# A planned single-core kernel gets new instruction costs, a clock for its DMAs, and other places for the first loads

## The chip, the cores and the metric

The kernel runs on one core of a Trainium2 chip. The metric is the device time of one execution in microseconds (us); smaller is better. TensorE (PE) multiplies, VectorE (DVE), ScalarE (ACT) and GpSimd (POOL) do the elementwise work, and SyncE (SP) issues every DMA.

## The reference

Two transformer-like blocks run one after the other on 512 tokens of width 2048, in float32. The first block: a memory of 256 rows is normalised and projected to keys and values; the tokens are normalised and projected to a gated delta-rule branch, to cross-attention queries and to a gate z; the gated result goes through an output projection and is added to the tokens. The second block does the same with an mLSTM and an HGRN2 branch, then adds `sigmoid(rmsnorm(h) @ w_pg) * (p @ w_pe)` and ends in a root-mean-square norm.

```python
mem_n = rms_norm(mem, mem_norm_g)
h = rms_norm(x, norm_g[i])
proj = jnp.einsum("bsd,de->bse", h, dn_w_in[j])
...
kv = jnp.einsum("bmd,de->bme", mem_n, w_kv)
...
y = jnp.concatenate([mix, xa], axis=-1) * jax.nn.silu(z)
x = x + jnp.einsum("bse,ed->bsd", y, w_out[i])
...
gate = jax.nn.sigmoid(jnp.einsum('bsd,de->bse', rmsnorm(h, pe_norm_w[l]), w_pg[l]))
h = h + gate * e
out = rmsnorm(h, final_norm_w)
```

## The kernel before, in words

Activations lie with features on the partitions and the 512 tokens along the free axis. A weight matrix is a list of jobs of 128 output columns each. A job's weights come in pieces of four 128x128 blocks (256 KB); ACT rounds a piece to `hi`, DVE takes the rest `lo`, and each block gives three matmuls (hi by the activation's high part, hi by its low part, lo by its high part) into one PSUM bank. Six raw pieces (`RAW`) may be on their way and five split pieces (`SPL`) may be ready.

No engine decides the order at run time. While the program is built, `Driver.run` plays a greedy planner: it keeps one clock for each engine (`clk`), adds a written cost for every instruction (`_on`), and emits the next instruction whose inputs are ready by these clocks, matmul units of the projections when nothing of higher priority is ready. Each engine then executes its own list strictly in this order, so an instruction that waits on the chip holds up all behind it on its engine. `calm` holds back optional work while ACT or DVE runs ahead of PE by the planner's clocks. All DMAs go out on SP's one queue, also in this order.

The opening. `first_loads` puts the eight loads of the memory (`mraw`, 256 KB each) after the first weight pieces and the sixteen loads of the tokens (`xraw`, 256 KB each) after the next sixteen. `mem_task` rounds the memory and sums its squares; `x_task` squares each token tile on ACT, adds it to `xsum` on DVE, and hands the normalised parts (`part`) to the query projection. The jobs of `w_k` come first, the first two of them interleaved piece by piece; then `w_v`, then `w_xq`. Until `w_xq` starts, PE multiplies with 256 columns of memory alone.

The middle. Twelve groups of the delta rule each need the inverse of eight 32x32 triangular blocks at once: `inverse` runs 31 steps on DVE, each a multiply and a `tensor_reduce` that needs it, then two transposes whose result `Dt` PE multiplies into tile `pp`. The planner gives a step's instructions these costs, and frees the engine for others after every third step.

The end. The jobs of `w_pg` fill the gate. For the last three tiles they are cut into two halves of 256 tokens, so that the final norm of the first half overlaps the matmuls of the second. `out_half` scales sixteen tiles: on POOL as a tensor_tensor for those of `on_pool`, whose weight ACT multiplied in before (`evac_g`), on DVE as a scalar_tensor_tensor for the rest.

Of the kernel before, what the change touches and what calls it, by code (L numbers as in the profile page):

```python
# [38 lines left out]
def v4(ap):  # L39
    return ap.rearrange("p (n c) -> p n c", n=NCH)  # L40

# [37 lines left out]
class Driver:  # L79
# [5 lines left out]
    def __init__(self, tc, wp, psp, sp):  # L85
        self.tc, self.nc, self.wp, self.psp, self.sp = tc, tc.nc, wp, psp, sp
        self.clk = dict(pe=0.0, act=0.0, dve=0.0, pool=0.0)
# [12 lines left out]
        self.nslot = 0  # L100
        self.table = None
        self.nhead, self.head = 0, None
# [8 lines left out]
    def act(self, out, in_, func, table=None, **kw):  # L111
        t = table or {AF.Exp: 1, AF.Ln: 1, AF.Silu: 2, AF.Sigmoid: 3}.get(func)
        cost = 0.11 + free_size(out) / 1200
        if t and t != self.table:
            self.table = t
            cost += 1.3
# [6 lines left out]
    def _v(self, eng, n):  # L123
        if eng is None:
            self._on("dve", 0.08 + n / 960, LV)
            return self.nc.vector
        self._on("pool", 0.1 + n / 400, LV)
        return eng

    def tt(self, out, a, b, op, eng=None):  # L130
        self._v(eng, free_size(out)).tensor_tensor(out=out, in0=a, in1=b, op=op)  # L131

    def stt(self, out, a, s, b, op0, op1):
        self._v(None, free_size(out)).scalar_tensor_tensor(out=out, in0=a, scalar=s, in1=b, op0=op0, op1=op1)  # L134

    def ts(self, out, a, s1, op0, s2=None, op1=None, eng=None):
        kw = dict(op1=op1) if op1 is not None else {}
        self._v(eng, free_size(out)).tensor_scalar(out=out, in0=a, scalar1=s1, scalar2=s2, op0=op0, **kw)

    def cp(self, out, a, eng=None):  # L140
        self._v(eng, free_size(out)).tensor_copy(out=out, in_=a)

    def set(self, out, v, eng=None):
        self._v(eng, free_size(out)).memset(out, v)

    def keep(self, out, in_, sign, fill):
# [5 lines left out]
        self._on("pool", 0.2 + n * c / 1200, LV)  # L152

    def scan(self, out, a, b, init, op0, op1):
        self._v(None, free_size(out)).tensor_tensor_scan(out=out, data0=a, data1=b, initial=init, op0=op0, op1=op1)

    def mm(self, out, lhsT, rhs, start=True, stop=True, tr=False):
        n = free_size(out)
        if lhsT.dtype == F32R:
            c = max(0.107, n / 2400)  # L160
        elif tr:
            c = 0.105
        else:
            c = max(0.055 if lhsT.shape[0] <= 32 else 0.107 if lhsT.shape[0] <= 64 else 0.2, n / 600)
            if lhsT.shape[0] <= 64:
                c = min(c, 0.107)
# [4 lines left out]
    def dma(self, out, in_, lat=2.3):  # L171
        self.nc.sync.dma_start(out=out, in_=in_)
        self.tau = max(self.tau, self.clk["pe"]) + lat
# [92 lines left out]
    def _pump(self):  # L266
        while self.i_dma < len(self.pieces):
# [6 lines left out]
            self.pieces[self.i_dma] = (j, c0, n, raw, max(self.clk["pe"] + 3.0, 4.5 + 1.5 * self.i_dma))  # L274
# [121 lines left out]
def build(ctx: ExitStack, tc: tile.TileContext, A, out):  # L396
# [49 lines left out]

    def first_loads(i):

        if i < len(mraw):
            nc.sync.dma_start(out=mraw[i], in_=A["memT"][:, 2 * i:2 * i + 2])  # L450
        elif i < len(mraw) + KT:
            k = i - len(mraw)
# [4 lines left out]
            d.give(f_x[k])  # L457
            f_x[k].tau = d.clk["pe"] + 3.0

    f_x = [Fut() for _ in range(KT)]  # L460
# [99 lines left out]
    def mem_task():  # L560
        hs = []
        for i, t in enumerate(mraw):
            d.tau = 3.8 + 1.5 * i
# [14 lines left out]
        for i, t in enumerate(mraw):  # L578
            d.tau = t0
            yield from d.calm(AHEAD)  # L580
# [10 lines left out]
    def x_task():  # L591
        ssum = yield from slot(name="xsum")
        for k, t in enumerate(xraw):
            yield from need(f_x[k])
            yield from d.calm(AHEAD)
# [6 lines left out]
            free(q)  # L602
        f = Fut()
# [135 lines left out]
    def evac_ab(job):  # L739
# [22 lines left out]
        d.dma(dgc, rows[0:32])  # L762
# [89 lines left out]
    def inverse(g, Mn):  # L852
# [273 lines left out]
    def y_loader():  # L1126
        yield from need(f_zb0)
        for i in range(KI):
# [8 lines left out]
            yield  # L1137
            d.dma(t, yscr[i])
            give((f_yl if i < 2 * XH else f_yf)[i], t)
        give(f_all)  # L1140
# [122 lines left out]
    def evac_if(job):  # L1263
# [35 lines left out]
        for j, r in enumerate((mu, wi, en)):  # L1299
            d.dma(drow[j], r[0:32], lat=0)  # L1300
        d.dma(dws, ws[:, 0:NCH])
# [8 lines left out]
        d.dma(wsb, bc(dws, 0, 128))  # L1310
# [29 lines left out]
    def ml_task(h):  # L1340
# [4 lines left out]
        for j in range(3):  # L1345
            t = yield from slot(name="rowb")
            yield
            d.dma(t, mlg["drow"][j, h:h + 1].broadcast_to((128, T)))
# [163 lines left out]
    def hg_task(h):  # L1512
# [39 lines left out]
        for l in range(len(LEVELS)):  # L1552
# [19 lines left out]
            elif LEVELS[l] == 1:  # L1572
# [3 lines left out]
                d._on("dve", 0.4, LV)  # L1576
# [114 lines left out]
    def on_pool(k):  # L1691
        return k % 3 == 1 and k < KT - NSP

    def evac_g(i):
        def gen(job):
# [37 lines left out]
    def out_half(c, n, t, last):  # L1733
# [3 lines left out]
        for k0 in range(0, KT, 2):  # L1737
            o = yield from slot((128, 2, n), name="out")
            te = []
            for k in (k0, k0 + 1):  # L1740
# [4 lines left out]
                if on_pool(k):  # L1745
                    tt(o[:, k - k0], h, t, MUL, eng=pool)
# [10 lines left out]
    d.nhead = len(mraw) + KT  # L1757
# [4 lines left out]
    d.add(jk[0], jk[1])  # L1762
    for j in jk[2:] + jv[:-2]:
# [246 lines left out]
```

## Time and profile before

| | us |
|---|---|
| median of 3 runs | 2913.86 |
| lowest and highest | 2908.96 and 2915.22 |
| the profiled execution, its own time | 2909.13 |
| its span from first to last instruction | 2907.3 |

The mean granted clock of TensorE over the span was 0.996 of full speed. A row of a view names the line of the helper that issues an instruction (L167 is every matmul, L120 every ACT instruction, L131 every tensor_tensor), so instructions are told apart by tiles. A square bracket at the end of a timeline row is the engine's idle time before the instruction, and what ended it.

### The profile page before, as it was taken

To read this page: it belongs to the slowest core of one execution; us is meant where nothing else is said; L and a number is where in the kernel's file an instruction comes from. 1 tells how busy PE (TensorE), PEld (TensorE's weight loads), DVE (VectorE), ACT (ScalarE), POOL (GpSimd) and SP (SyncE) were. 2 spreads that over 40 slices of the span, in tenths; PEclk is the share of its full clock that TensorE was granted. 3 is DMA by queue.
4 is the path that set the end of the run, shared out by engine and by line. 5 is a ranking of instruction groups with operands and counts; after the bars stand their busy time and mean duration, and the time that the engine had idled before them with its cause. 6 is when DMAs were issued, how large, how long until landed. Compare 5 with 4: busy or idle time off the path is not lost. (4 is left out here: it accounts for less than half of the span.)

```text
span 2907.3 us, 41141 instructions
## 1 busy us (share of the span) xinstructions
PE 2856.6 (98%) x15032; PEld 2390.5 (82%) x15032; DVE 1722.0 (59%) x3305; ACT 1395.3 (48%) x2636; POOL 81.0 (3%) x180
## 2 busy tenths in 40 slices
PE   8999999999999999999999999999999999999997
PEld 7877887788788888888888878888888888888887
DVE  6746677778777777635333364455655655544446
ACT  6544545555445555435222334445555556433434
POOL 0000100100000100000000000000000000000000
PEclk9999999999999999999999999999999999999999
DMA  7422422233222222354433433222222222333324
GB/s 244 142 80 93 123 93 90 95 101 96 82 93 99 95 98 92 100 168 129 129 118 120 148 110 109 87 81 80 84 80 80 89 86 87 115 119 112 96 94 145
DMA packets 179021, 311.05 MB, mean 107 GB/s; under 512 B 25345, under 2 KB 32129, under 8 KB 178817
## 3 DMA queue, kind: packets, MB, share of 16 engines
q1 hardware_dynamic: 178816, 308.41, 33.4%
q8 instruction: 118, 1.93, 0.3%
q14 instruction: 87, 0.70, 0.1%
HBM read 292.34 MB, written 15.99 MB: 106 GB/s over the span
## 5 line engine op out<-in xcount | busy, mean ns | idle before, releaser
L131 DVE TENSOR_TENSOR lo<-raw,hi 128x512 fp32r<-128x512 f32 (+1 forms) x956 | 643.9, 685 | 618.5 <-ACT hi L120 599.5
L120 ACT ACTIVATE hi<-raw 128x512 fp32r<-128x512 f32 (+1 forms) x964 | 591.6, 621 | 865.0 <-PE acc L167 761.8
L167 PE MATMUL acc<-xh,hi 128*128 128x512 f32 x1424 | 582.4, 409 | 0.7 <-ACT xh L120 0.4
L167 PE MATMUL acc<-xl,hi 128*128 128x512 f32 x1424 | 556.2, 391 | 2.8 <-DVE xl L131 2.7
L167 PE MATMUL acc<-xh,lo 128*128 128x512 f32 x1408 | 551.5, 392 | 4.5 <-DVE lo L131 4.4
L167 PE MATMUL acc<-x2h,hi 128*128 128x512 f32 x1040 | 415.8, 400 | 0.0
L167 PE MATMUL acc<-x2l,hi 128*128 128x512 f32 x1040 | 405.2, 390 | 0.0
L167 PE MATMUL acc<-x2h,lo 128*128 128x512 f32 x1024 | 399.8, 390 | 0.0
L167 PEld LDWEIGHTS acc<-xh,lo 128*128 128x128 f32 x1408 | 264.4, 188 | 63.7 <-DVE lo L131 6.2
L167 PEld LDWEIGHTS acc<-xl,hi 128*128 128x128 f32 x1424 | 268.5, 189 | 54.6 <-DVE xl L131 3.9
L167 PEld LDWEIGHTS acc<-xh,hi 128*128 128x128 f32 x1424 | 268.2, 188 | 53.6 <-issue 1.7
L167 PE MATMUL acc<-ph,hi 128*128 128x512 f32 x768 | 298.8, 389 | 0.0
L167 PE MATMUL acc<-pl,hi 128*128 128x512 f32 x768 | 298.8, 389 | 0.0
L167 PE MATMUL acc<-ph,lo 128*128 128x512 f32 x768 | 298.8, 389 | 0.0
L167 PEld LDWEIGHTS acc<-x2h,lo 128*128 128x128 f32 x1024 | 192.2, 188 | 41.4
L167 PEld LDWEIGHTS acc<-x2h,hi 128*128 128x128 f32 x1040 | 195.6, 188 | 37.2
L167 PEld LDWEIGHTS acc<-x2l,hi 128*128 128x128 f32 x1040 | 195.7, 188 | 36.9
L167 PEld LDWEIGHTS acc<-pl,hi 128*128 128x128 f32 x768 | 144.2, 188 | 30.0
L167 PEld LDWEIGHTS acc<-ph,hi 128*128 128x128 f32 x768 | 144.2, 188 | 29.9
L167 PEld LDWEIGHTS acc<-ph,lo 128*128 128x128 f32 x768 | 144.2, 188 | 29.8
L134 DVE SCALAR_TENSOR_TENSOR cv<-acc,c_dn_conv,cv 128x511 f32<-128x511 f32 x144 | 107.4, 747 | 35.6 <-ACT cv L120 32.1
L131 DVE TENSOR_TENSOR Xb<-Xb,Nb 128x16 f32<-128x16 f32 (+30 forms) x372 | 115.4, 310 | 8.8
(322 smaller groups left out, 3679.8 us busy)
## 6 DMA issues: line engine op xcount, KB each, us to landing
raw<-w_qkv SPq DMA_DIRECT2D x192, 256.0 KB, 3.2
raw<-w_out SPq DMA_DIRECT2D x192, 256.0 KB, 2.9
raw<-w_z SPq DMA_DIRECT2D x128, 256.0 KB, 3.2
raw<-w_pg SPq DMA_DIRECT2D x76, 256.0 KB, 3.1
gR<-dgc SPq DMA_DIRECT2D x48, 256.0 KB, 4.1
raw<-w_k SPq DMA_DIRECT2D x32, 256.0 KB, 4.7
raw<-w_v SPq DMA_DIRECT2D x32, 256.0 KB, 3.6
raw<-w_xq SPq DMA_DIRECT2D x32, 256.0 KB, 3.1
```

The lines of the kernel that those rows point to most:

```text
L120: self.nc.scalar.activation(out=out, in_=in_, func=func, **kw)
L131: self._v(eng, free_size(out)).tensor_tensor(out=out, in0=a, in1=b, op=op)
L134: self._v(None, free_size(out)).scalar_tensor_tensor(out=out, in0=a, scalar=s, in1=b, op0=op0, op1=op1)
L167: self.nc.tensor.matmul(out, lhsT=lhsT, rhs=rhs, start=start, stop=stop, is_transpose=True if tr else None)
```

## The change

The planner's costs are written anew: ACT from PSUM is cheaper and with a per-partition scale dearer; DVE's scalar_tensor_tensor and scan are dearer, its copies and tensor_scalar from SBUF cheaper, its reduce in the inverse cheaper; POOL is split by instruction; a 512-column projection matmul costs 544/2400 us in place of 512/2400, and a switch between small and large matmuls costs 0.15 us. A clock for SP and one for the DMA engines (`land`) say when a load is there; before, a load was taken to be there 2.3 or 3.0 us after PE's clock. The loads of memory and tokens are placed in a list (`loads`) that starts the tokens after the fifth weight piece, between the memory's loads. The first four jobs of `w_k` are interleaved in place of two. The token squares are added on POOL. `y_loader` no longer waits in the planner for one load before it issues the next. At the end, ACT multiplies the final weight into all thirteen whole tiles, so that DVE scales them with tensor_tensor, and one more tile (the thirteenth) goes to POOL.

```diff
-        cost = 0.11 + free_size(out) / 1200
+        cost = (0.055 if in_psum(in_) else 0.105) + free_size(out) / 1200
+        if not all(isinstance(kw.get(k, 0.0), (int, float)) for k in ("scale", "bias")):
+            cost += 0.075
...
     def tt(self, out, a, b, op, eng=None):
-        self._v(eng, free_size(out)).tensor_tensor(out=out, in0=a, in1=b, op=op)
+        n = free_size(out)
+        self._v(eng, 0.07 + n / 960, 0.43 + n / 590).tensor_tensor(out=out, in0=a, in1=b, op=op)
...
         if lhsT.dtype == F32R:
-            c = max(0.107, n / 2400)
+            c = max(0.107, (n + 32) / 2400)
...
+        if small != self.small_mm:
+            self.small_mm = small
+            c += 0.15
...
+    def land(self, n=128 * T, extra=0.1):
+
+        t = max(self.clk["pe"], self.clk["sp"])
+        self.clk["sp"] = t + 0.5
+        self.dq = max(self.dq, t + 2.0)
+        self.dq += (0.7 if self.dq > 9 else 1.1) * n / (128 * T)
+        return self.dq + 0.25 + extra
...
+    loads = [[] for _ in range(1 + 3 * KT)]
+    for i in range(len(mraw)):
+        loads[4 * (i // 2) + (i % 2 if i < 2 else i % 2 - 1)].append(("m", i))
+    n = 0
+    for i in range(len(loads)):
+        if n < KT and (i % 4 in (1, 2) and i > 4 if i < KT else i >= KT):
+            loads[i].append(("x", n))
+            n += 1
...
             if k == 0:
-                cp(ssum, q)
+                cp(ssum, q, eng=pool)
             else:
-                tt(ssum, ssum, q, ADD)
+                tt(ssum, ssum, q, ADD, eng=pool)
...
-        d._on("dve", 1.2, LV)
+        d._on("dve", 2.0, LV)
...
             nc.vector.tensor_reduce(out=Xb[:, :, i], in_=pr[:, :, 0:i + 1], op=ADD, axis=AX.X)
-            d._on("dve", 0.33 + 8 * (i + 1) / 960, LV)
+            d._on("dve", 0.07 + 8 * (i + 1) / 960, LV)
...
     def on_pool(k):
-        return k % 3 == 1 and k < KT - NSP
+        return k % 3 == 1 and k < KT - NSP or k == KT - NSP - 1
...
-                if on_pool(i):
-                    act(h, h, AF.Copy, scale=w[:, i:i + 1])
+                act(h, h, AF.Copy, scale=w[:, i:i + 1])
...
-                if on_pool(k):
-                    tt(o[:, k - k0], h, t, MUL, eng=pool)
+                if k < KT - NSP:
+                    tt(o[:, k - k0], h, t, MUL, eng=pool if on_pool(k) else None)
...
-    d.add(jk[0], jk[1])
-    for j in jk[2:] + jv[:-2]:
+    d.add(*jk[:4])
+    for j in jk[4:] + jv[:-2]:
```

## Rows read from the trace of the kernel before

**Rows 1.** The page: the span, and busy time of each engine.
```profile
span 2907.3 us, 41141 instructions
...
PE 2856.6 (98%) x15032; PEld 2390.5 (82%) x15032; DVE 1722.0 (59%) x3305; ACT 1395.3 (48%) x2636; POOL 81.0 (3%) x180
```

**Rows 2.** PE's waits, 0 to 131 us: total, times, longest.
```profile
PE acc L167 <- ACT mh L120: 7.1, 1, 7.1
PE acc L167 <- DVE lo L131: 3.9, 2, 2.7
PE acc L167 <- ACT hi L120: 2.5, 1, 2.5
PE acc L167 <- DVE xl L131: 1.9, 1, 1.9
```

**Rows 3.** Windows of the opening: each engine's busy time (instructions), clock, DMA.
```profile
10.00:20.00 10.00, 7.54 (x53) 7.34 (x51) 5.77 (x12) 5.81 (x13) 0.00 (x0) 0.95 0.92 309
20.00:30.00 10.00, 10.00 (x62) 9.78 (x62) 9.79 (x18) 9.88 (x20) 0.00 (x0) 0.71 0.95 332
30.00:40.00 10.00, 8.79 (x74) 8.58 (x73) 7.03 (x13) 6.29 (x12) 0.00 (x0) 1.00 0.80 259
40.00:50.00 10.00, 7.25 (x58) 6.84 (x57) 6.21 (x15) 7.32 (x17) 0.00 (x0) 0.99 0.64 218
50.00:60.00 10.00, 10.00 (x73) 10.00 (x74) 8.36 (x16) 4.70 (x9) 0.00 (x0) 0.84 0.65 213
60.00:70.00 10.00, 10.00 (x86) 10.00 (x85) 7.20 (x15) 6.66 (x13) 0.00 (x0) 1.00 0.51 155
```

**Rows 4.** Timeline around the first token tile: SP's issue, then ACT.
```profile
15.22 0.33 SPq L456 DMA_DIRECT2D xraw<-xT  x1
...
18.33 0.63 ACT L120 ACTIVATE xsq<-xraw 128x512 f32<-128x512 f32 x1 [3.51 <-DMA xraw<-xT]
```

**Rows 5.** Windows of the middle: columns as above (PE, PEld, DVE, ACT, POOL).
```profile
325.00:1207.00 882.00, 869.70 (x5259) 720.98 (x5258) 685.13 (x1558) 476.25 (x1031) 63.23 (x143) 1.00 0.29 94
...
1700.00:2500.00 800.00, 794.81 (x3960) 667.39 (x3959) 456.09 (x775) 407.35 (x687) 4.71 (x12) 1.00 0.28 87
```

**Rows 6.** PE's waits, 131 to 2880 us: one row of eleven.
```profile
PE acc L167 <- DVE xl L131: 0.8, 1, 0.8
```

**Rows 7.** Timeline of DVE, an inverse: start, duration, instruction.
```profile
561.47 0.25 DVE L131 TENSOR_TENSOR Xb<-Xb,Nb 128x88 f32<-128x88 f32 x1
561.76 0.25 DVE L881 TENSOR_REDUCE Xb<-Xb 128x8 f32<-128x88 f32 x1
562.04 0.26 DVE L131 TENSOR_TENSOR Xb<-Xb,Nb 128x96 f32<-128x96 f32 x1
```

**Rows 8.** Timeline of DVE and PE where that inverse ends.
```profile
591.37 0.45 DVE L900 STREAM_TRANSPOSE Dt<-Dt 128x256 f32<-128x256 f32 x1
...
591.91 0.57 PE L167 MATMUL pp<-Dt,gR 32*32 32x32 f32 x25 [0.48 <-issue]
```

**Rows 9.** PE's waits, 2880 us to the end.
```profile
PE ss L167 <- DVE gt L131: 2.6, 1, 2.6
PE acc L167 <- DVE lo L131: 2.0, 1, 2.0
```

**Rows 10.** Timeline of POOL and DVE: the final scaling, and a lone tensor_tensor pair.
```profile
2881.73 2.83 POOL L131 TENSOR_TENSOR out<-h1r,gt 128x256 f32<-128x256 f32 x4 [390.25 <-ACT gt L120]
2896.40 3.31 POOL L131 TENSOR_TENSOR out<-h1r,gt 128x256 f32<-128x256 f32 x4 [11.84 <-ACT gt L120]
...
2888.49 4.04 DVE L134 SCALAR_TENSOR_TENSOR out<-h1r,c_fin_w,gt 128x256 f32<-128x256 f32 x10
...
2896.35 6.80 DVE L134 SCALAR_TENSOR_TENSOR out<-h1r,c_fin_w,gt 128x256 f32<-128x256 f32 x12 [0.86 <-ACT gt L120]
...
40.10 0.75 DVE L131 TENSOR_TENSOR xk<-acc,mraw 128x256 f32<-128x256 f32 x2
```

More of the change, by code (lines that the diff above doesn't have):

```diff
@@ L40, in v4, with in_psum @@
     return ap.rearrange("p (n c) -> p n c", n=NCH)
+def in_psum(ap):
+    return ap.tensor.space == "PSUM"
 def free_size(ap):
@@ L101, in __init__ @@
         self.table = None
+        self.small_mm = False
         self.nhead, self.head = 0, None
@@ L151, in keep @@
             compare_op=ALU.is_ge if sign > 0 else ALU.is_gt, fill=fill)
-        self._on("pool", 0.2 + n * c / 1200, LV)
+        self._on("pool", 0.1 + n * c / 1050, LV)
     def scan(self, out, a, b, init, op0, op1):
-        self._v(None, free_size(out)).tensor_tensor_scan(out=out, data0=a, data1=b, initial=init, op0=op0, op1=op1)
+        self._v(None, 0.07 + free_size(out) / 460, 0).tensor_tensor_scan(
+            out=out, data0=a, data1=b, initial=init, op0=op0, op1=op1)
     def mm(self, out, lhsT, rhs, start=True, stop=True, tr=False):
         n = free_size(out)
+        small = max(lhsT.shape[0], free_size(lhsT)) <= 64
         if lhsT.dtype == F32R:
-            c = max(0.107, n / 2400)
+            c = max(0.107, (n + 32) / 2400)
         elif tr:
-            c = 0.105
-        else:
-            c = max(0.055 if lhsT.shape[0] <= 32 else 0.107 if lhsT.shape[0] <= 64 else 0.2, n / 600)
-            if lhsT.shape[0] <= 64:
-                c = min(c, 0.107)
+            c = 0.109
+        elif small:
+            c = 0.035 if lhsT.shape[0] <= 32 else 0.11
+        else:
+            c = max(0.222, (n + 5) / 600)
+        if small != self.small_mm:
+            self.small_mm = small
+            c += 0.15
         self.nc.tensor.matmul(out, lhsT=lhsT, rhs=rhs, start=start, stop=stop,
@@ L169, in mm, with dma @@
         self._on("pe", c, LP)
-    def dma(self, out, in_, lat=2.3):
+    def land(self, n=128 * T, extra=0.1):
[4 more added lines that the diff above has]
+        return self.dq + 0.25 + extra
+    def dma(self, out, in_, extra=0.9, n=128 * T):
         self.nc.sync.dma_start(out=out, in_=in_)
-        self.tau = max(self.tau, self.clk["pe"]) + lat
+        self.tau = max(self.tau, self.land(n, extra))
     def slot(self, shape=(128, T), dt=F32, name="s", reserve=0):
@@ L273, in _pump @@
             self.nc.sync.dma_start(out=raw[:, :n, :j.w.shape[2]], in_=j.w[:, c0:c0 + n])
-            self.pieces[self.i_dma] = (j, c0, n, raw, max(self.clk["pe"] + 3.0, 4.5 + 1.5 * self.i_dma))
+            self.pieces[self.i_dma] = (j, c0, n, raw, self.land(n * 128 * j.w.shape[2]))
             self.i_dma += 1
@@ L445, in build @@
         xraw.append(d.slot_now(name="xraw"))
-    def first_loads(i):
[L449 to L452, printed above, removed]
+    loads = [[] for _ in range(1 + 3 * KT)]
[6 more added lines that the diff above has]
+            n += 1
+    def first_loads(i):
+        for what, k in loads[i] if i < len(loads) else ():
+            if what == "m":
+                nc.sync.dma_start(out=mraw[k], in_=A["memT"][:, 2 * k:2 * k + 2])
+                f_m[k].tau = d.land()
+                f_m[k].done = True
+                continue
             if k == 0:
@@ L456, in first_loads @@
             nc.sync.dma_start(out=xraw[k], in_=A["xT"][:, k])
-            d.give(f_x[k])
-            f_x[k].tau = d.clk["pe"] + 3.0
+            f_x[k].tau = d.land(extra=0.5)
+            f_x[k].done = True
+    f_m = [Fut() for _ in mraw]
     f_x = [Fut() for _ in range(KT)]
@@ L562, in mem_task @@
         for i, t in enumerate(mraw):
-            d.tau = 3.8 + 1.5 * i
+            d.tau = 0.0
+            yield from need(f_m[i])
             yield
@@ L579, in mem_task @@
             d.tau = t0
+            yield from need(f_m[i])
             yield from d.calm(AHEAD)
@@ L592, in x_task @@
         ssum = yield from slot(name="xsum")
+        tp = 0.0
         for k, t in enumerate(xraw):
+            d.tau = 0.0
             yield from need(f_x[k])
+            yield
             yield from d.calm(AHEAD)
@@ L761, in evac_ab @@
         yield
-        d.dma(dgc, rows[0:32])
+        d.dma(dgc, rows[0:32], n=32 * T)
         pt = yield from transpose4(rows)
@@ L1756, in build @@
     d.head = first_loads
-    d.nhead = len(mraw) + KT
+    d.nhead = len(loads) - 1
     d.spawn(mem_task(), 1)
```

38 lines of the change are left out of this document (24 added, 14 removed).

## The prediction, made before the changed kernel ran

> **What bounds the kernel now.** I read the page first: PE is busy for 2856.6 us of a span of 2907.3 us [rows 1]. The change leaves the matmuls as they are, in number and shape, so it can only win what PE stands idle or runs slowly, some 50 us in all, and it can lose without such a limit. The next view is therefore PE's waits, by stretch, with the windows beside them. They fall into four places.
>
> The first 7.1 us are the wait for the first loads [rows 2]; they stay, since the first load of memory and the first weights go out as before.
>
> The opening behind it: with the memory's 256 columns a window of 10 us holds 86 matmuls when nothing is short (60 to 70 us), 0.116 us each. The five windows before it hold 53, 62, 74, 58 and 73 [rows 3]; 130 are missing, 15 us at that price, less the matmuls that PE was still too cold to make early in the first window. The window at 20 us has no idle time at all and still holds only 62: the granted clock there is 0.71, so part of the stretch ran at the lower of the two levels (1.2 in place of 2.4 GHz), right behind PE's wait of 2.5 us. A wait here is paid nearly twice.
>
> The middle, 325 to 2500 us: PE is idle for 882.0 - 869.7 = 12.3 us and 800.0 - 794.8 = 5.2 us [rows 5], single waits of at most a few us, 17.5 us together.
>
> The end: two waits of 2.6 and 2.0 us [rows 9], and then the final scaling, 6.8 us on DVE after PE's last result [rows 10].
>
> **Part 1, where the first loads stand.** The wait of 2.5 us is for `hi`, and the reason stands on ACT: the square of the first token tile was put in front of it, the tile's load was issued at 15.22 us, and ACT stood 3.51 us until 18.33 us for it [rows 4]. The planner had taken the load to be there 3.0 us after PE's own clock, which runs ahead of a loaded DMA queue. With `land` the square is emitted by a clock that counts the loads in front of it, and the first tokens go out after the fifth weight piece. I take this wait as gone with the slow clock behind it: 2.5 us and 24 missing matmuls x 0.116 = 2.8 us, together 5.3 us.
>
> From 30 to 60 us 12 + 28 + 13 = 53 matmuls are missing, 6.2 us. These are two waits for `lo` [rows 2], 3.9 us, and the slow clock behind the second (0.84). They come from the evacuation of the key jobs, whose norm DVE waits for with `lo` queued behind it. The change leaves `evac_k` alone and, with four jobs that end together, puts two such norms close to each other; against that, four jobs use each memory tile for twice the work before PE needs the next. Bounds 0 and 6.2; I credit 2.7, a little under half.
>
> Four interleaved jobs ask less of the DMA, not nothing. Up to the sixteenth weight piece 16 + 8 + 6 = 30 loads of 256 KB go out. At 332 GB/s and a DMA share of 0.95, what the busiest window shows, one takes 0.79 us and thirty 23.7 us, while PE has 192 matmuls x 0.116 = 22.3 us of work. So DMA stays just the slower; I charge 1.5 us.
>
> The tokens must be ready for `w_xq`. Now PE waits 1.9 and 0.8 us for `xl` [rows 2, 6]. In the plan DVE is freed of sixteen adds, and PE's written cost is 6% higher (544 against 512), so optional work passes `calm` earlier. But PE will also come there earlier. Bounds 0 and 2.7; I credit 1.8.
>
> **Part 2, the token sums on POOL.** The end of the kernel shows what two engines do to each other. POOL alone takes 2.83 / 4 = 0.71 us for a 256-column tensor_tensor, beside DVE 3.31 / 4 = 0.83. DVE alone takes 4.04 / 10 = 0.40 us for its scaling; of the last twelve, eight at 0.40 leave 3.6 us for the four that meet POOL, 0.90 each [rows 10]. So one POOL instruction of 256 columns costs DVE 0.5 us, one of 512 an estimated 1.0, and sixteen 16 us; the adds that leave DVE were worth 16 x 0.75 = 12 us (0.75 us is the pair of 256 columns in rows 10). DVE ends up with 4 us more, not less, inside a stretch where it was busy 9.79 of 10 us once [rows 3]. The five split pieces in reserve are worth 5 x 12 x 0.116 = 7 us of PE, so I charge nothing beyond the 1.5 us; without that reserve it is the rival B.
>
> The Trainium skill (SBUF — State Buffer, Who interferes with whom) says that a DVE instruction with two SBUF inputs and a GpSimd instruction that reads SBUF exclude each other, the second blocked until the first is finished. By that rule DVE's instruction would take 0.40 + 0.71 = 1.11 us where the trace has 0.90, and the sixteen sums would cost DVE 23 us in place of 16; the direction agrees, the size is smaller here.
>
> **Part 3, the written costs.** They move no work, only the order. For most instructions the direction is plain from the diff. One goes astray. In the inverse a multiply and the reduce behind it took 562.04 - 561.47 = 0.57 us for 88 elements [rows 7], each waiting for the one before. The old costs say 0.08 + 0.33 + 2 x 88/960 = 0.59, the new ones 0.14 + 0.18 = 0.32. Over 31 steps the planner will hold DVE free 7.7 us too early. What takes this up: after each third step it waits 0.3 us for the result, then for the end of a unit of three matmuls (0.68 us, on average half of it), some 0.6 us x 10 = 6 us, if no other work fills these gaps; DVE is busy for 685 of 882 us there. So at the end of an inverse DVE is late by about 2 us, at most 7.7. There is no reserve behind it: `Dt` ended at 591.82 and PE began `pp` at 591.91 [rows 8], having waited for it. What is late there stops PE. Against 2 us stand the coarser steps of everything else; I charge 0.7 us for each of twelve inverses, 8 us, with bounds 0 and 12 x 4 = 48. The 17.5 us of idle time in the middle come from the old plan's errors, and a new order removes some and makes others: credit 6, bounds 0 and 17.5. The middle: +2 us.
>
> **Part 4, the end.** DVE's ten scalings of the first half stand in front of the `gt` that PE's last sum waits for; as tensor_tensor they cost 0.375 in place of 0.40 us, and one fewer is left, about 0.4 us. After the last sum POOL has five tiles, 5 x 0.83 = 4.15 us, in which DVE makes 4.6 of its eleven; the other 6.4 (three of them at 0.40) take 2.5 us: 6.65 against 6.80. The wait of 2.0 us for `lo` depends on where that piece falls in DVE's list; I credit 0.5 (bounds 0 and 2.0). Together -1.1 us. The nine added products on ACT, 9 x 0.63 = 6 us, lie beside `w_pg` matmuls, with ACT busy for 48% of the span; without that cover they cost these 6 us. The burst of `y` loads that the planner now allows takes SP's queue, but weights are fetched six pieces ahead; nothing.
>
> **The sum.** Opening -5.3 - 2.7 - 1.8 + 1.5 = -8.3; middle +2; end -1.1: -7.4 us. The profiled execution took 2909.1 us, so 2901.7 by its scale; the median of the runs shown is 4.7 us above it, and against the median I say 2906.5.
>
> **The rivals.** A, slower: the short-costed inverse. If DVE is late by 3 us at each, PE loses 36 us, and with the other terms (-8.3, -6, -1.1) the kernel takes 2913.9 + 20.6 = 2934.5. It decides from 15.4 / 12 = 1.3 us an inverse upwards. For it: rows 7 and 8. Against it: PE's waits of now for `pp` are 0.5 us, and the gaps of rows 5. B, no change: POOL's sums hold `lo` back in the opening, where DVE has no room, and PE's waits come back in another place with their slow clock; the opening gives 2 us: 2912.8. For it: 9.79 us busy; against: the windows from 30 us on, with DVE at 6 to 8. C, more: nearly all waits of the middle vanish as well: -8.3 - 15 - 1.1 = 2889.5. For it: these waits are faults of the plan; against: an instruction planned to be just in time has no reserve. D, the clock doesn't do what it says: `land` counts 0.7 us a load where the window shows 0.79, so after 46 loads it is 4 us early and ACT again stands before a token tile; the opening gives 3 us: 2911.8.
>
> **How the numbers follow.** Forecast 0.46 (its own range 2900 to 2912.5), A 0.24, B 0.10, C 0.14, D 0.06. About 0.2% (6 us) is what a measurement of this kernel can tell from no change. Faster by more: C and four fifths of the forecast, 0.51; within it: B, D and the rest of the forecast, 0.25; slower: A, 0.24. The range 2888 to 2932 leaves out the far part of A and a little of C.
>
> **What would show it.** Right: no ACT idle time on a token load before 25 us; 75 or more matmuls in the windows from 20 us on, clock near 1; the first `w_xq` matmul some 8 us earlier; POOL busy about 20 us more; DVE instructions of 0.9 us beside it. Wrong: new waits of PE for `pp`, `up` or `pst` on DVE between 325 and 1207 us, more than 12.3 us of idle time there (A); waits for `lo` before 60 us as long as now (B, D).

## The result and the profile after

The changed kernel is slower: a median of 2939.65 us (2939.21 to 2941.61) against 2914.54 us for the kernel before, a ratio of 1.0093 with a 95% interval of 1.0078 to 1.0108. The forecast was 2906.5 in a range of 2888 to 2932; the time lies outside it, on the other side of the kernel before. Rival A (2934.5) came nearest. The marks below are read from one profiled execution of each kernel. Executions of one and the same kernel differ by up to 8 us, so a difference of a few us between two marks says little by itself.

The profiled execution has a span of 2938.1 us, 30.8 more than before (the medians differ by 25.1; the profiled execution of before was one of its shorter ones). The page after, span and busy time, answers to [rows 1]:

```profile
span 2938.1 us, 41167 instructions
...
PE 2872.2 (98%) x15032; PEld 2391.4 (81%) x15032; DVE 1710.6 (58%) x3287; ACT 1391.3 (47%) x2638; POOL 100.3 (3%) x198
```

The matmuls are as many as before, DVE and ACT are busy for a little less, POOL for 19.3 us more. So the 30.8 us are time in which PE stood or ran slowly. To find the place I cut both traces at marks: the first matmul of tokens (`acc<-xh`, the start of `w_xq`), the first of the gated result (`acc<-ph`, the start of the output projection, behind the last delta-rule group), the first of the second block's tokens (`acc<-x2h`), the first of `p @ w_pe` (`acc<-p_h`), the first of `w_pg` (`acc<-x3h`), and the last matmul. Two rows of the summary by tile, after, where "120.1 to 124.7" are the first and last start in the window of the view; the first starts are the marks:

```profile
L186 PE MATMUL acc<-xh,hi x7: 389/395/477, 120.1 to 124.7; 128*128 128x512 f32 x7
...
L186 PE MATMUL acc<-ph,hi x5: 389/389/389, 1373.0 to 1375.7; 128*128 128x512 f32 x5
```

The same marks stand at 116.6 and 1339.0 us before. That gives this table (us; the third column is the difference of the two marks, and it is what the experiments call the delta stage):

| | first `xh` | delta stage | `ph` to `x2h` | `x2h` to `p_h` | `x3h` to last matmul | behind it |
|---|---|---|---|---|---|---|
| before | 116.6 | 1222.4 | 348.2 | 1003.1 | 202.1 | 12.2 |
| after | 120.1 | 1252.9 | 348.1 | 1003.0 | 199.5 | 11.8 |
| difference | +3.5 | +30.5 | -0.1 | -0.1 | -2.6 | -0.4 |

(From `p_h` to `x3h` it is 2.7 us in both.) Nearly the whole loss is the delta stage, with the opening's 3.5 us beside it and 3.0 us won at the end. PE's waits after, from 131 to 1400 us (total, times, longest):

```profile
PE pst L186 <- DVE ud L140: 11.1, 13, 2.8
PE pp L186 <- issue: 8.1, 9, 1.1
PE kq L186 <- ACT cv L128: 4.3, 1, 4.3
PE ks L186 <- DVE S L143: 3.0, 6, 0.6
PE up L186 <- DVE rp L143: 2.1, 5, 0.8
```

Before, the same list had 0.5 us for `pp` and one wait of 3.2 for `ud`; `ks` and `up` did not stand in it, and the wait of `kq` for `cv` was 0.2. Now many short waits line up along the recurrence: the inverse's product `pp`, then the state's products `ks`, `up` and `pst`. How one begins is seen on DVE's and PE's timeline at the end of an inverse, after (compare [rows 8]):

```profile
1138.59 1.28 DVE L140 TENSOR_TENSOR lo<-raw,hi 128x512 fp32r<-128x512 f32 x2
1139.79 0.62 DVE L944 STREAM_TRANSPOSE Dt<-Xb 128x256 f32<-128x256 f32 x1
1140.45 0.45 DVE L946 STREAM_TRANSPOSE Dt<-Dt 128x256 f32<-128x256 f32 x1
...
1141.00 0.69 PE L186 MATMUL pp<-Dt,gR 32*32 32x32 f32 x32 [1.07 <-issue]
```

`Dt` ends at 1140.90 and PE, idle for 1.07 us, begins 0.10 us later. In 11 of the 12 inverses after, PE begins `pp` 0.10 us behind `Dt`; before, it came between 0.1 and 7.8 us behind it, and stood for it in one. The planner now places `pp` where it believes the inverse to be done, and the chip is not there yet.

The windows after, which answer to [rows 3] and [rows 5] (columns as there):

```profile
325.00:1207.00 882.00, 850.48 (x5072) 691.65 (x5071) 657.45 (x1518) 459.87 (x1000) 60.12 (x143) 1.00 0.29 91
1700.00:2500.00 800.00, 796.45 (x3968) 669.10 (x3968) 461.24 (x786) 408.95 (x697) 4.04 (x12) 1.00 0.28 89
...
20.00:30.00 10.00, 7.91 (x56) 7.71 (x55) 7.40 (x11) 8.48 (x18) 3.92 (x3) 0.86 0.98 351
30.00:40.00 10.00, 10.00 (x83) 10.00 (x82) 9.38 (x17) 6.60 (x13) 0.00 (x0) 0.97 0.95 326
40.00:50.00 10.00, 10.00 (x86) 10.00 (x85) 7.44 (x14) 7.83 (x16) 4.35 (x3) 1.00 0.79 279
50.00:60.00 10.00, 7.84 (x53) 7.46 (x52) 7.14 (x17) 7.85 (x19) 0.00 (x0) 0.83 0.33 101
60.00:70.00 10.00, 9.69 (x81) 9.48 (x80) 4.05 (x7) 6.52 (x13) 7.34 (x6) 1.00 0.50 163
70.00:80.00 10.00, 5.70 (x29) 5.16 (x30) 4.66 (x10) 3.86 (x9) 3.43 (x3) 0.66 0.16 52
```

In the same 882 us PE makes 5072 matmuls in place of 5259. At 882 / 5259 = 0.168 us each, a mean over large and small ones, the missing 187 are worth about 31 us, the whole loss of the stage, while PE's listed idle time there grew by only 31.5 - 12.3 = 19.2 us. The count of matmuls tells more than the idle time. In the opening two windows (30 to 50 us) are nearly as full as they can be, and one is nearly empty: 29 matmuls from 70 to 80 us. The timelines of ACT, DVE, POOL and PE there:

```profile
73.62 0.63 ACT L128 ACTIVATE qh<-xsum 128x512 fp32r<-128x512 f32 x1 [6.29 <-POOL xsum L140]
...
64.24 1.44 DVE L140 TENSOR_TENSOR lo<-raw,hi 128x512 fp32r<-128x512 f32 x1 [1.63 <-ACT hi L128]
74.28 0.69 DVE L140 TENSOR_TENSOR ql<-xsum,qh 128x512 fp32r<-128x512 f32 x1 [8.60 <-ACT qh L128]
...
62.27 11.32 POOL L140 TENSOR_TENSOR xsum<-xsum,xsq 128x512 f32<-128x512 f32 x8 [14.54 <-ACT xsq L128]
...
74.30 0.80 PE L186 MATMUL ss<-qh,ones_r 128*128 128x512 f32 x1 [4.62 <-ACT qh L128]
75.62 0.41 PE L186 MATMUL acc<-mh,hi 128*128 128x256 f32 x1
...
78.52 0.28 PE L186 MATMUL acc<-mh,lo 128*128 128x256 f32 x1
```

POOL adds the last eight token squares in 11.32 us, 1.42 each on average. ACT's next instruction is the split of that sum; ACT stands for it for 6.29 us with weight pieces queued behind, DVE stands 8.60 us for ACT, and PE 4.62 us. Then PE runs at the lower level for some 4 us more (0.41 us a row in place of 0.28; the records of the clock have it low from 71.6 for 6.8 us).

### The profile page after: what moved, and what is told of

Its sections match the earlier page's. It is cut to its first block, busy times and chain, and to the rows that moved or that the text cites. A ratio compares the mean times of both kernels' runs of the same rounds, so it can differ in the third digit from the quotient of the medians.

```text
span 2938.1 us, 41167 instructions
## 1 busy us (share of the span) xinstructions
PE 2872.2 (98%) x15032; PEld 2391.4 (81%) x15032; DVE 1710.6 (58%) x3287; ACT 1391.3 (47%) x2638; POOL 100.3 (3%) x198
## 3 DMA queue, kind: packets, MB, share of 16 engines
q8 instruction: 118, 1.93, 0.3%
```

## The experiments

Theory A is rival A: the inverse's written cost is too short. Its first rival, P, puts the loss on the dearer projection matmul (544 in place of 512), by which DVE's and ACT's optional work is let through at other times. For the opening, S1 says that what POOL's token sums cost is ACT's standing in its list, S2 that it is DVE's `lo` running slowly beside POOL; J4 says that the four interleaved key jobs win about what the opening wins where the sums stay on DVE. All times below are medians, ratios are against the kernel before on the same chip with 95% intervals, and the marks are read as in the table above.

### The reduce's cost, both ways

`e1_reduce_033` puts the old cost of the reduce back into the changed kernel; `e3_before_reduce_007` puts the new one into the kernel before.

```diff
-            d._on("dve", 0.07 + 8 * (i + 1) / 960, LV)
+            d._on("dve", 0.33 + 8 * (i + 1) / 960, LV)
```

> The changed kernel with one constant put back: the reduce in the inverse costs 0.33 us + n/960 in the plan again, not 0.07. Theory A (the planner holds DVE free 7.7 us too early in each of twelve inverses, and PE, in its fixed order, waits for what DVE has not done): the stage from the first xh matmul to the first ph matmul, 1252.9 us now and 1222.4 before, falls to 1220 to 1235 and the kernel to 2910 to 2922; the waits of PE for ud and Dt, 11 and 8 us, fall under 5 together. Rival P (the reserve went with the 6% dearer projection matmul): the stage stays within 6 us of 1253.

Measured: 2913.05 us, 1.0006 [0.9997, 1.0015]; first `xh` 122.6, delta stage 1224.1. The stage and the total are as theory A said. The waits for `ud`, `pp` and `Dt` are not under 5 us together: 6.1 for `ud`, 0.3 and 0.2 for the others.

> The kernel before with one constant changed: the reduce costs 0.07 us + n/960. Theory A alone: the stage grows from 1222.4 by 15 to 30 us and the kernel with it, to 2930 to 2945. Rival P: the old matmul cost still gives its reserve, so the stage grows by less than 8 us.

Measured: 2938.77 us, 1.0096 [1.0079, 1.0113]; first `xh` 115.5, delta stage 1251.5. PE's waits from 131 to 1400 us, first of the changed kernel with the old cost:

```profile
PE p L186 <- DVE XA L154: 7.0, 3, 3.7
PE pst L186 <- DVE ud L140: 6.1, 7, 1.5
...
PE pp L186 <- issue: 0.3, 1, 0.3
```

and of the kernel before with the new one:

```profile
PE pst L167 <- DVE ud L131: 6.8, 7, 3.0
PE p L167 <- DVE XA L141: 3.5, 2, 3.1
PE up L167 <- DVE rp L134: 2.8, 6, 0.6
PE ks L167 <- DVE S L134: 2.4, 7, 0.4
PE pp L167 <- DVE Dt L900: 2.2, 5, 0.5
```

One constant takes 28.8 us of the stage away in the one kernel and puts 29.1 us into the other, and the row of waits for `up`, `ks` and `pp` goes and comes with it. A holds. P is not needed: with 512 still written, the kernel before loses as much. The waits show only a part of the loss, and other waits take the place of some of them (7.0 us for `XA`).

### PE's written cost

`e2_pe_512` puts the old matmul cost into the changed kernel, `e9_033_dve_pe512` into the changed kernel with reduce and token sums put right (`e5_033_dve`, below), and `e12_before_pe544` puts the new one alone into the kernel before.

```diff
-            c = max(0.107, (n + 32) / 2400)
+            c = max(0.107, n / 2400)
```

> The changed kernel with one constant put back: a projection matmul costs n/2400 us in the plan, not (n + 32)/2400. Rival P (PE's old, too low cost was a reserve of 6%, and without it everything planned to be just in time comes late): the stage falls from 1252.9 to 1220 to 1235 and the kernel to 2910 to 2922. Theory A: the reserve gives back 6% of the stretches in which DVE is late, 3 us of some 50 in each inverse: between 5 and 20 us, the waits for Dt not gone.

Measured: 2921.12 us, 1.0036 [1.0023, 1.0049]; delta stage 1237.9.

> Both repairs (reduce at 0.33, sums on DVE; 2903.7 us) and the projection matmul at n/2400 again. It asks whether the 15 us that the old matmul cost gave beside the wrong reduce were a cover for that error or a gain of its own. Cover: with the reduce right nothing is left, the stage from the first xh to the first ph matmul stays within 4 us of 1223.8 and the total within 6 of 2903.7. Own gain: the stage falls to 1205 to 1216, the kernel under 2896.

Measured: 2906.44 us, 0.9981 [0.9972, 0.9991]; delta stage 1227.5, against 1223.8 in `e5_033_dve`.

> The kernel before with one constant changed: a projection matmul costs (n + 32)/2400 us in the plan. Rival P (the lost reserve hurts by itself): the stage grows from 1222.4 by 8 us or more and the kernel by as much. Theory A: with DVE's costs right it stays within 5 us.

Measured: 2893.67 us, 0.9941 [0.9926, 0.9956]; first `xh` 113.9, delta stage 1210.3. Its waits from 131 to 1400 us, whole but for four entries of 0.4 us or less:

```profile
PE pst L167 <- DVE ud L131: 3.8, 3, 2.6
PE acc L167 <- DVE lo L131: 1.7, 1, 1.7
```

With the short reduce, the smaller matmul cost wins 15 us of the stage. A reason would be that PE's clock is then too early as well as DVE's; no run shows that apart. With the longer reduce the smaller cost wins nothing (`e9`), so the 15 us only covered the short reduce. In the kernel before, the larger matmul cost alone wins 12.1 us of the stage. Both theories missed that: P had a loss of 8 us or more, A no change beyond 5. So P is turned around: put alone into the kernel before, 544 wins 18 us by the medians, more than the whole change does with its two faults put right (`e5_033_dve`). Why it wins there is not shown beyond the waits that are gone.

### Between the two costs, above them, and a finer form

`e7_020_dve` and `e11_045_dve` write 0.20 and 0.45 for the reduce (token sums on DVE). `e10_chain_dve` leaves the changed kernel's 0.07 and adds to every DVE instruction that needs the result of the one before it what that costs:

```diff
         dep = self._dep if (e, self.tau) == self._last else self.tau
+        if e == "dve" and (e, self.tau) == self._last:
+            cost += 0.11
```

> Token sums on DVE and the reduce at 0.20 us + n/960, half way. Theory A, with the size of the error as the cause: the planner is 3.7 us too early in each inverse and not 7.7, the stage lies between 1224 and 1252, 1230 to 1242; the span of an inverse lies between 42 and 50 us. If the loss of the changed kernel was one unlucky order, there is no such course: the stage may lie anywhere from 1220 to 1255.

Measured: 2909.83 us, 0.9993 [0.9984, 1.0002]; delta stage 1230.9; an inverse takes 43.9 us from its first transpose to its last reduce, on average.

> Sums on DVE and the reduce dearer than it is, 0.45 us + n/960. Theory A says that only a cost that is too low hurts, since PE then stands for DVE, while one that is too high only starts work later that PE does not wait for: the stage stays within 4 us of 1223.8. If the stage goes on falling with the cost (0.07: 1252, 0.20: 1231, 0.33: 1224), reserve in general is what is worth something: under 1218.

Measured: 2905.76 us, 0.9981 [0.9972, 0.9991]; delta stage 1228.0, 4.2 us above 1223.8 and so just outside the 4 us.

> The reduce stays at 0.07 us + n/960 as in the change, sums on DVE; in its place every DVE instruction that the planner places right behind the one whose result it continues costs 0.11 us more. Theory A in its finer form (the new costs are those of independent instructions in a row, and what is missing is the time by which a dependent one starts later): the stage falls from 1252.1 to 1220 to 1230, as with 0.33, the span of an inverse is 47 to 54 us, the kernel 2900 to 2908. If only the reduce's own constant matters by chance of order, the stage lies anywhere up to 1252.

Measured: 2899.23 us, 0.9961 [0.9947, 0.9975]; delta stage 1222.6, an inverse 48.2 us, both inside what was expected; the total is 1 us below. With 0.07, 0.20, 0.33 and 0.45 the stage takes 1252.1, 1230.9, 1223.8 and 1228.0 us: half the error costs only a quarter of the loss, and too long a cost does little. That is a course and not one unlucky order. The finer form, which leaves the reduce alone and prices dependence, does as well as 0.33.

### The token sums

`e4_sums_dve` takes the token sums of the changed kernel back to DVE; `e5_033_dve` does so with the reduce at 0.33; `e6_033_pool_yield` keeps them on POOL, with the reduce at 0.33, and lets the planner place other work ahead of the split of the sum (the last hunk, which is its own).

```diff
-                cp(ssum, q, eng=pool)
+                cp(ssum, q)
             else:
-                tt(ssum, ssum, q, ADD, eng=pool)
+                tt(ssum, ssum, q, ADD)
...
         d.tau = tp
+        yield
         f = Fut()
```

> The changed kernel with the token sums on DVE again, all else kept. Theory S (in the opening ACT stands 6.3 us for the chain of POOL's sums, with the rounding of weights behind it; PE's wait of 4.6 us and its slow clock of 6.8 us come from that): the first xh matmul goes from 120.1 to 111 to 114 us and the kernel to 2930 to 2934. Rival K (the opening is lost by four key jobs that end together, the sums are harmless): the first xh matmul stays within 2 us of 120. The stage behind it is the same in both.

Measured: 2929.54 us, 1.0066 [1.0051, 1.0081]; first `xh` 111.8, delta stage 1252.1. The sums on POOL had cost 120.1 - 111.8 = 8.3 us of the opening.

> The changed kernel with both repairs: reduce at 0.33 us + n/960 in the plan, token sums on DVE. If the two faults are separate, the gains add: 2939.7 - 26.6 - 10.1 = 2903, a ratio to the kernel before of 0.996 to 0.998; first xh matmul at 111 to 114 us, the stage from there to the first ph matmul 1222 to 1228. If the gain of one was order by chance, 2910 to 2916.

Measured: 2903.71 us, 0.9971 [0.9960, 0.9983]; first `xh` 112.1, delta stage 1223.8. The two faults add up: by the medians the sums cost 9.3 us here (against `e1_reduce_033`) and 10.1 with the short reduce (`e4_sums_dve` against the changed kernel). Its windows:

```profile
20.00:30.00 10.00, 9.44 (x77) 9.10 (x77) 8.31 (x15) 8.00 (x16) 0.00 (x0) 1.00 1.01 341
30.00:40.00 10.00, 9.86 (x78) 9.26 (x77) 8.34 (x14) 7.75 (x16) 0.00 (x0) 1.00 1.00 359
40.00:50.00 10.00, 7.70 (x60) 7.32 (x60) 6.58 (x13) 6.33 (x13) 0.00 (x0) 1.00 0.67 226
50.00:60.00 10.00, 8.52 (x66) 8.12 (x67) 8.08 (x17) 7.70 (x19) 0.00 (x0) 1.00 0.44 133
60.00:70.00 10.00, 10.00 (x86) 10.00 (x85) 7.37 (x16) 7.45 (x17) 0.00 (x0) 1.00 0.65 210
```

The clock is 1.00 throughout; from 40 to 60 us 46 matmuls are missing still.

> The reduce at 0.33 us, the token sums left on POOL, and one yield in front of the rounding of the finished sum, so that the planner emits it when it holds the sum for finished and not at once. Theory S1 (the loss was ACT standing in its order for POOL's chain): ACT's wait for the sum falls from 6.3 us to under 2, the first xh matmul comes at 111 to 115 us, total near that of the run with the sums on DVE. Theory S2 (POOL and DVE in each other's way is the loss): the wait moves but the first xh matmul stays at 118 to 123.

Measured: 2908.93 us, 0.9990 [0.9981, 0.9999]; first `xh` 118.4. DVE's timeline, a row of the summary by tile (ns: least, median, most) and a window of it:

```profile
71.01 6.35 DVE L140 TENSOR_TENSOR lo<-raw,hi 128x512 fp32r<-128x512 f32 x5
...
L140 DVE TENSOR_TENSOR lo<-raw,hi x5: 678/1759/1774, 71.0 to 76.7; 128x512 fp32r<-128x512 f32 x5
...
70.00:80.00 10.00, 7.35 (x52) 6.30 (x51) 9.75 (x12) 5.19 (x11) 5.37 (x4) 1.00 0.36 126
```

ACT no longer stands (0.82 us for the sum), and the window from 70 us holds 52 matmuls in place of 29. But now DVE is the one that is full: five `lo` take 6.35 us, three of them beside POOL's adds (the median is 1.76 us). The last two take 0.60 and 0.68, which leaves 5.07 / 3 = 1.69 us from start to start for the three. The kernel before has five without POOL, 0.60 each:

```profile
63.17 3.09 DVE L131 TENSOR_TENSOR lo<-raw,hi 128x512 fp32r<-128x512 f32 x5
```

The first `xh`, 118.4, lies in the range named for S2 and outside that for S1, but neither alone is right. `e1_reduce_033` differs from this kernel by the yield alone and has its first `xh` at 122.6: without ACT's stand it comes 4.2 us earlier. The other 118.4 - 112.1 = 6.3 us come back only when the sums leave POOL (`e5_033_dve`). Of these the three `lo` account for 3 x 1.09 = 3.3 us of DVE's time; the rest is not divided, since other windows changed as well (35 matmuls from 50 to 60 us, 47 in `e1_reduce_033`).

### Two key jobs in place of four

```diff
-    d.add(*jk[:4])
-    for j in jk[4:] + jv[:-2]:
+    d.add(*jk[:2])
+    for j in jk[2:] + jv[:-2]:
```

> Both repairs, and only the first two key jobs interleaved as before. Theory J4 (four jobs use each memory tile for twice the work and take the DMA off the path): the first xh matmul comes 2 to 6 us later than with four, 114 to 118. Rival (four key jobs that end together cost in evacuation what the DMA gives): within 2 us of the run with four, or earlier.

Measured: 2907.44 us, 0.9984 [0.9975, 0.9994]; first `xh` 116.8 against 112.1 in `e5_033_dve`. PE's waits up to 131 us, whole but for one of 0.3 us:

```profile
PE acc L186 <- ACT mh L128: 12.6, 3, 7.3
```

J4 holds: the four jobs are worth 4.7 us, all that the opening won. With two, the new places of the loads gain nothing over the kernel before: the token loads now stand between the memory's, and PE waits 12.6 - 7.3 = 5.3 us more for memory tiles. The four jobs hide that. Against `e12_before_pe544` (old places, two jobs, first `xh` 113.9) the new places come out 2.9 us later, with other costs changed as well. Four jobs with the loads in their old places were not run.

### What is left of the stage

`e5_033_dve` has all of the change but its two faults, and a stage of 1223.8 us; the kernel before with the matmul cost alone has 1210.3. About 13 us were unexplained. Four theories: E, the other costs of ACT, DVE and POOL; M, those of small matmuls and the switch; W, the clock of the weights' landing; D, that of the other loads, with `y_loader` no longer waiting. All start from `e5_033_dve`. `e13_old_act_dve` writes the old costs of E, `e14_old_small_mm` those of M, `e15_old_both` both; `e16_old_dma` undoes D on top of that, `e17_old_raw` undoes W, `e18_old_dma_raw` D and W.

```diff
-        cost = (0.055 if in_psum(in_) else 0.105) + free_size(out) / 1200
-        if not all(isinstance(kw.get(k, 0.0), (int, float)) for k in ("scale", "bias")):
-            cost += 0.075
+        cost = 0.11 + free_size(out) / 1200
...
-        self._v(None, 0.13 + free_size(out) / 960, 0).scalar_tensor_tensor(
+        self._v(None, 0.08 + free_size(out) / 960, 0).scalar_tensor_tensor(
```

> Both repairs (2903.7 us, stage 1223.8), and ACT's, DVE's and POOL's costs as in the kernel before; PE's costs, the DMA clock, the four key jobs and the loads of the change stay. Theory E (the new elementwise costs lose the 12 to 14 us that the old kernel with the new projection cost alone has over this one, since they are those of instructions that need not wait for the one before): stage 1208 to 1215, total 2888 to 2895. Rival M (the costs of the small matmuls and the switch lose them): stage within 4 us of 1223.8.

Measured: 2910.69 us, 0.9998 [0.9989, 1.0008]; delta stage 1230.1. E fails; with the old costs the stage is 6 us longer, not shorter. That is more than the 4 us that rival M allowed, too.

```diff
-        elif small:
-            c = 0.035 if lhsT.shape[0] <= 32 else 0.11
...
-        if small != self.small_mm:
-            self.small_mm = small
-            c += 0.15
```

> Both repairs, and the costs of transposes, small and float32 matmuls as in the kernel before, without the switch's 0.15 us; the rest of the change stays. Theory M: stage 1208 to 1215. Theory E: within 4 us of 1223.8.

Measured: 2898.78 us, 0.9958 [0.9943, 0.9973]; delta stage 1225.6. M fails for the stage.

> Both of the last two: of the written costs only the projection matmul's is new, with the new loads, the DMA clock, the four key jobs and the end. If E or M or both together hold the loss, the stage is 1208 to 1213 as in the old kernel with that one cost, the first xh matmul at 110 to 113, total 2885 to 2892. If the DMA clock or the y loads hold it, the stage stays above 1220.

Measured: 2903.22 us, 0.9969 [0.9956, 0.9981]; delta stage 1225.8. So E and M together do not hold it either. Its longest waits from 131 to 1400 us:

```profile
PE pst L181 <- DVE ud L138: 7.6, 3, 2.9
PE acc L181 <- DVE lo L138: 2.5, 3, 2.0
```

```diff
         self.nc.sync.dma_start(out=out, in_=in_)
-        self.tau = max(self.tau, self.land(n, extra))
+        self.tau = max(self.tau, self.clk["pe"]) + 2.3
...
-            t0 = d.tau
             d.dma(t, yscr[i])
             give((f_yl if i < 2 * XH else f_yf)[i], t)
-            d.tau = t0
```

> As the run with all old costs but the projection matmul's (stage 1225.8), and the loads other than weights are again taken to be there 2.3 us after PE's clock, the y loads one behind the other. Theory D (these loads' clock holds the 15 us to the old kernel with the new projection cost): stage 1208 to 1214, total 2886 to 2893. Rival W (the weights' clock holds them): stage 1221 to 1230. Rival Z (any of these plans with the reduce about right lies somewhere between 1210 and 1230, and no single cost decides it): anywhere in that band, without the two runs of this call adding up.

Measured: 2893.67 us, 0.9936 [0.9922, 0.9951]; first `xh` 112.5, delta stage 1212.1. D holds: 13.7 us of the stage; the total lies 0.7 us above what was expected. The waits from 131 to 1400 us, whole but for five entries of 0.4 us or less, are nearly those of `e12_before_pe544`:

```profile
PE pst L181 <- DVE ud L138: 3.7, 3, 2.6
PE acc L181 <- DVE lo L138: 1.7, 1, 1.7
```

```diff
-            self.pieces[self.i_dma] = (j, c0, n, raw, self.land(n * 128 * j.w.shape[2]))
+            self.pieces[self.i_dma] = (j, c0, n, raw, self.clk["pe"] + 3.0 if self.i_dma >= 64
+                                       else self.land(n * 128 * j.w.shape[2]))
```

> As the run with all old costs but the projection matmul's, and the weights, from the sixty-fifth piece on, are again taken to be there 3.0 us after PE's clock. Theory W: stage 1208 to 1214. Theory D: 1221 to 1230. Rival Z: anywhere in the band.

Measured: 2904.49 us, 0.9971 [0.9959, 0.9982]; delta stage 1226.6. W fails.

> Both of the last two: of the change only the projection matmul's cost, the loads and the four key jobs of the opening and the end are left. If the DMA clock in either form holds it: stage 1208 to 1213 and, with the first xh matmul at 110 to 113 us, a total of 2885 to 2891. If it stays at 1220 or more, the place where the opening hands over is enough to make another plan of the stage, and the 1210 was a lucky one.

Measured: 2894.11 us, 0.9937 [0.9923, 0.9952]; delta stage 1210.2. The stage is where D put it; the total lies 3 us above what was expected. Rival Z is not borne out: the plans with the old clock of the other loads and 544 (`e12`, `e16`, `e18`) have stages of 1210.2 to 1212.1 us whatever their opening, those with the new clock and a reduce of 0.33 have 1223.8 to 1230.1.

`e16_old_dma`, `e18_old_dma_raw` and `e12_before_pe544` are the fastest versions found and not told apart, 0.6% faster than the kernel before and 1.6% faster than the changed one (by the two ratios, 0.9936 / 1.0093 = 0.984). Which half of D costs the time, the landing time of the other loads or the `y` loads, was not tried apart. PE's idle time above 0.15 us in the stage is 13.1 us in `e15` and 6.8 in `e16`, mostly waits for `ud` and `lo`; why the plan with the new clock makes them stays open.

## Why the prediction was wrong

**The step that failed** is in Part 3: "I charge 0.7 us for each of twelve inverses, 8 us". The mechanism stood there, and with it its sign: DVE is held free 7.7 us too early, there is no reserve behind `Dt`, and what is late stops PE. Its size was 28.8 to 29.1 us, 2.4 us an inverse, beyond the 1.3 from which rival A decides and short of the 3 at which it was priced. What was wrong is that lateness is paid once, at `pp`. PE's listed waits for `pp` are 8.1 us (0.5 before), about the 8 us charged; `ud`, `S` and `rp` behind it have 16.2 us of waits of their own (3.2 before, 6.1 for `ud` alone in `e1`), and a part of the loss shows in no list of waits. The other assumption, that gaps of the plan would take up 6 of the 7.7 us, is left in doubt: from the first transpose to the last reduce an inverse took 53.7 us on average before, with DVE idle for 16% of it (8.4 us), and 42.2 us after, with 9% (3.8 us). But `e7` has 43.9 us and 9% too and loses a quarter, so shrunken gaps alone do not make the loss. The other term there, a credit of 6 for waits that a new order would remove, was met along the path below by the matmul's cost (-12.1), which had been given no term of its own in the middle; that it came out is luck.

**A term that was missing**: the new clock of the DMAs outside the opening was charged nothing ("The burst of `y` loads ... nothing"), and with the landing time of the other loads it cost 13.7 us (`e15` against `e16`).

With these the stage adds up along the kernels that were run: before 1222.4; matmul cost alone, -12.1 (`e12`); new opening and the rest of `e16`, +1.8; DMA clock, +13.7 (`e15`); new costs of ACT, DVE and small matmuls, -2.0 (`e5`); reduce, +28.3 (`e4`); sums on POOL, +0.8. Together +30.5, the difference of the table. Each is the difference of two plans, and plans with the reduce at 0.33 and the new DMA clock scatter by several us (1223.8 to 1230.1), so the terms of 1 and 2 us are not causes. Rival A named the mechanism, but its total came near partly by luck: it had the opening at -8.3 us, where it was +3.5, and had no term for the DMA clock.

**Part 1** was right about the first load: ACT's stand of 3.51 us [rows 4] is 0.21 us now (12.63, `xsq<-xraw`). Rival D's mechanism is out. One sum there is wrong and enters nothing else: of five windows at 86 the 320 matmuls leave 430 - 320 = 110 missing, 12.8 us, not 130 and 15. Of the -8.3 us the opening gave 4.5 to 4.8 where the sums did not spoil it (`e5`, `e4`), and `e8` shows that without the four jobs nothing of it is left. The waits for `xl`, 2.7 us that lie behind the first `xh` before, are gone after as credited; by the marks they belong to the stage. The credit of 2.7 for `lo` was not met: in `e5` PE waits 2.7 us for `lo` in place of 3.9, and adds 1.6 for the token sum.

**Part 2** failed in its charge of nothing. It looked at DVE's busy time, which sixteen sums change by 4 us, and held five split pieces against it. It did not ask who waits for the last sum: ACT, in order, with the splits of the weight pieces behind it. The kernel emits the split of the sum right behind the last square, so ACT stands for what is left of POOL's chain; that the planner wrote 0.43 + 512/590 = 1.30 us for an add that took 1.42 is only 1 of the 6.29 us. 8.3 us of the opening were lost. That is rival B's place with more than its price, and by another way: of the sixteen meetings that were charged, the changed kernel has four in which a DVE instruction took longer (two `lo` of 1.44 us, two `ml` of 1.5 and 1.6). The price of one meeting was right: the estimate was 1.0 us for an instruction of 512 columns, and `e6` has 1.69 from start to start against 0.60 alone, 1.09 more. POOL alone takes 1.33 (changed kernel, DVE standing):

```profile
66.92 6.67 POOL L140 TENSOR_TENSOR xsum<-xsum,xsq 128x512 f32<-128x512 f32 x5
```

The Trainium skill (SBUF — State Buffer, Who interferes with whom) has the second instruction blocked until the first is finished; that would be 0.60 + 1.33 = 1.93 us for a pair. The trace has 1.69 us for a pair, so here too the direction agrees and the size is smaller.

**Part 4** had -1.1 us and got -3.0: the wait of 2.0 us for `lo` [rows 9] is gone, which had been credited with 0.5 and may as well have come back, and only `gt` is left, 2.2 us. The gain in front of that wait was put at 0.4 us; its own prices give 4.04 - 9 x 0.375 = 0.67. The scaling behind the last sum was sized rightly:

```profile
2927.58 4.41 POOL L140 TENSOR_TENSOR out<-h1r,gt 128x256 f32<-128x256 f32 x5 [11.84 <-ACT gt L128]
...
2927.54 5.41 DVE L140 TENSOR_TENSOR out<-h1r,gt 128x256 f32<-128x256 f32 x8 [0.47 <-ACT gt L128]
2932.87 1.26 DVE L143 SCALAR_TENSOR_TENSOR out<-h1r,c_fin_w,gt 128x256 f32<-128x256 f32 x3
```

From 2927.54 to 2934.13 are 6.6 us, where 6.65 were worked out; three of the eight at 0.35 leave 4.36 for the five beside POOL, 0.87 each (0.90 in the text).

**The signs named ahead**: new waits for `pp`, `up` and `pst`, and more than 12.3 us of idle time in the 882 us (31.5), as said for A. Of the signs of being right, POOL's 20 us more came (19.3). The windows from 20 us on did not keep 75 matmuls or the clock (56 at 0.86, 53 at 0.83, 29 at 0.66), and the first `w_xq` matmul came 3.5 us later in place of some 8 earlier. The sign of B and D did not show: up to 60 us PE waits 2.1 us for `lo`, 3.9 before.

## What to carry to other kernels

In a planner for engines that run in order, the cost of an instruction that needs the result of the one just before it is another number than its cost in a stream; written too short, it was paid here at several later meeting points and not once. Before new costs go in together, put each alone into the old kernel: here one constant lost 28 us, another won 18 by the median, and the changed kernel, 25 us slower, hid what each did. When an operation moves to a slower engine, ask first which engine waits in order for its last result, and what is queued behind that.

## What the runs showed of the hardware

The cost of dependence on DVE can be read off one place, DVE's timeline at the end of the changed kernel, with instructions of 256 columns:

```profile
2920.70 0.42 DVE L140 TENSOR_TENSOR h1r<-h1r,gt 128x256 f32<-128x256 f32 x1
2921.16 0.42 DVE L140 TENSOR_TENSOR gt<-h1r 128x256 f32<-128x256 f32 x1
2921.62 0.42 DVE L140 TENSOR_TENSOR ssum<-ssum,gt 128x256 f32<-128x256 f32 x1
2921.96 1.76 DVE L140 TENSOR_TENSOR out<-h1r,gt 128x256 f32<-128x256 f32 x5
```

The first three each need the one before and start 0.46 us apart; five that need nothing of each other take 1.76 / 5 = 0.35. The difference, 0.11 us, is what `e10_chain_dve` added.

Beside POOL, DVE fell to one instruction for each of POOL's, at both sizes: 0.87 us against POOL's 0.88 with 256 columns, 1.69 with 512. Alone DVE takes 0.35 and 0.60 and POOL 0.71 and 1.33, so a pair takes more than POOL alone and less than the sum of both.

PE's listed waits understate what many short stalls cost. In the stage idle time above 0.15 us rose from 15.2 to 31.6 us, 16.4 of the 30.5 lost. The clock explains little of the rest: its records have two stretches of 3.4 us at the lower level in the stage after, one before. A matmul of 512 columns is recorded with 0.39 us at a pitch of 0.23 us, so a stall of up to 0.16 us behind it does not show; that this makes up the remainder is argued, not shown.
